# Fixed PSUM tiles for transposes, and an early load of the neighbourhood bias

## The chip, the cores and the metric

The kernel runs on one core of one Trainium2 chip. The metric is the device time of the whole program in microseconds (us), the median of the runs shown. Instructions run on five engines with a queue each: TensorE (PE in the profile; PEld is its weight load), VectorE (DVE), ScalarE (ACT), GpSimd (POOL) and SyncE (SP, which here issues all DMAs).

## What is computed

Two stacks of two transformer layers follow each other on 256 tokens of 1024 numbers, in float32. A layer of the first stack is a feed-forward, a mixer of four attentions, and a second feed-forward:

```python
for l in range(DEPTH):                       # DEPTH = 2
    h = rms_norm(x, ffn1_norm[l])
    x = x + 0.5 * swiglu(h, ffn1_w_gate[l], ffn1_w_up[l], ffn1_w_down[l])
    h = rms_norm(x, mix_norm[l])
    ...
    o_a = neighborhood_attention(na_q, na_k, na_v, ..., na_rel_bias[l], rows)
    o_b = diff_attention(...)
    o_c = gqa_axial_attention(...)
    o_d = dilated_attention(...)
    x = x + concatenate([o_a, o_b, o_c, o_d]) @ w_out[l]
    h = rms_norm(x, ffn2_norm[l])
    x = x + 0.5 * swiglu(h, ffn2_w_gate[l], ffn2_w_up[l], ffn2_w_down[l])
```

The neighbourhood attention adds a learned bias to its scores. The bias depends on the distance in rows and columns of a grid 64 wide, and only keys within a window of 16 columns count. A layer of the second stack is another mixer of three attentions and one feed-forward, with norms whose scale and shift come from a product of a vector with a large matrix ("modulation", loaded as `ada`).

## The kernel before

**Products.** Every weight matrix is streamed from HBM in units of 128 x 2048 numbers (`WStream`, lines 396 to 467). SP loads a unit into one of three buffers `raw`. ACT casts it to a rounded high part `whi`, and DVE subtracts to get the low part `wlo`; four pairs of them exist, and a unit is split when the fourth unit before it is done. PE then forms each product as three matmuls (`mm3`, line 625): high by high, low by high and high by low. So each load has a lead over its use of several units.

**Feed-forward** (`ffn`, line 641). The inner width of 2816 is done in 11 chunks of 256 (`NCH`). For each chunk and each half of the tokens, PE makes a gate and an up projection into one PSUM tile `mm` (two of them exist), ACT applies the gate function (`sil`), DVE multiplies (`hch`), PE transposes `hch` into a PSUM tile `tp` (`turn`, line 658), ACT and DVE split it into `hth` and `htl`, and the down projection of the chunk four before (`down`, line 671) accumulates into four PSUM tiles `y`. Between these steps `slot` advances background work: constants, a bias of the second stack, and the modulation, 192 loads of 256 KB `ada` with a DVE operation each.

**First kind of mixer** (`mixer1`, line 1088). `inproj` (line 1033) makes six chunks of projections. Each chunk of queries and keys goes through `prep` (line 847): ACT copies and squares, DVE sums, a power on POOL gives the norm's factor (`rs<-ms`), DVE scales and rotates, PE transposes into `tp`, ACT and DVE split that into `qkT`. When inputs are ready, jobs begin: `diff_job` (line 971, four heads) and `job` (line 903, two heads each of the dilated, grouped and neighbourhood attention, in this order). A job makes scores into PSUM tiles called `att` (they take slots of `y`, and of `mm` during the output projection), DVE takes maxima or adds a bias (`nm`, `e`), ACT exponentiates (`p`, `pd`), PE transposes through `tp` and multiplies by the values. `outproj` (line 1059) ends the mixer.

**The neighbourhood bias.** `na_bias` (line 826) takes four tiles `nab` of 128 x 512, one a head, and issues for each of them four loads on SP; a load fills 64 partitions with four runs of 64 numbers (256 bytes) each, 64 KB. `mixer1` calls it after the first two chunks of projections (`pre2`, line 1095). `na_bias_mask` (line 840) multiplies each tile by 8 and adds the mask of the window, one DVE operation a tile; it is a job of its own ahead of the two neighbourhood jobs (line 1135). `job` reads the tiles when it adds the bias (line 923).

**The order.** The kernel's Python code doesn't issue instructions at once. `Plan` (line 73) collects them with what each depends on (`add`, line 100), an estimated cost (`cost`, line 165: an issue on SP counts 475 ns) and the tiles with a limited number of slots that it touches. `order` (line 196) then simulates the five engines: of the operations that can start within 60 ns of the earliest, each engine takes the one of the highest priority, and `slot_time` (line 240) says whether the slots for the tiles of an operation are free and may be taken ahead of tiles that come earlier in the program. Priorities come from a pass from the end backwards, three times over (`priorities`, line 324). `issue` (line 318) emits the instructions in the order found. A DMA may not be issued ahead of the last matmul that stands before it in the program (line 136), the weight loads excepted. Each engine runs its own queue in that order and waits wherever an input is late, so a late input holds what is queued behind it.

**Tiles.** PSUM has eight banks: two `mm`, two `tp`, four `y`. `tp` (line 617) takes a tile of the pool's rotating slots. SBUF has 20 tiles `m` of 512 numbers (`NMID`) for all intermediate values, `nab` and `ada` among them.

```python
    def tp(self):
        return self.ps.tile([P, 512], F32, tag="tp", name="tp")
```

All instructions are emitted by `issue`, so they carry its line, L322, in the profile; they are told apart by the names of their tiles.

Of the kernel before, what the change touches and what calls it, by code (L numbers as in the profile page):

```python
# [72 lines left out]
class Plan:  # L73
# [3 lines left out]
    def __init__(self, nc):  # L77
        self.nc = nc
        self.ops, self.slot_of, self.slots = [], {}, {}
        self.write, self.read = {}, {}  # L80
        self.last_mm = self.cold = None
        self.lead = []
        for e in ("tensor", "vector", "scalar", "gpsimd", "sync"):
            setattr(self, e, Engine(self, e))
# [15 lines left out]
    def add(self, eng, method, args, kw):  # L100
# [4 lines left out]
        for writes in (False, True):  # L105
            for k, a in aps:
# [13 lines left out]
                if not writes:  # L120
                    if a.space == PSUM:
                        deps.update(j for j, _ in self.read[name] if self.ops[j][0] != eng)
# [42 lines left out]
    def cost(self, eng, method, args, kw, aps):  # L165
# [4 lines left out]
        psum = any(a.space == PSUM for _, a in aps)  # L170
# [25 lines left out]
    def order(self, prio):  # L196
# [43 lines left out]
        def slot_time(i):  # L240
# [3 lines left out]
            for t in ops[i][5]:  # L244
                if t not in live:
                    k = self.slot_of[t]
                    q = queue[k]
                    while head[k] < len(q) and q[head[k]] in done_alloc:
                        head[k] += 1
                    c = need.get(k, 0)  # L250
                    if free[k] <= c or place[t] > head[k] and max(held[k][head[k]:place[t]]) + c >= self.slots[k]:
                        return None
                    need[k] = c + 1
                    t0 = max(t0, sorted(freed_at[k])[c])
# [63 lines left out]
    def issue(self):  # L318
        for i in self.order(self.priorities())[0]:
            eng, method, args, kw = self.ops[i][:4]  # L320
            for m, a, k in args if method == "fused" else [(method, args, kw)]:
                getattr(getattr(self.nc, eng), m)(*a, **k)  # L322
# [147 lines left out]
class Net:  # L470
    def __init__(self, ctx, tc, A, out, stop):
# [20 lines left out]
        self.ps = pool("ps", 2, space=PSUM)  # L492
        self.mhalf = self.const.tile([P, 64], F32, name="mhalf")
# [123 lines left out]
    def tp(self):  # L617
        return self.ps.tile([P, 512], F32, tag="tp", name="tp")
# [22 lines left out]
    def ffn(self, ydone, mid, pre, r=None):  # L641
# [63 lines left out]
        for c in range(2, NCH):  # L705
            u = [W.next() for _ in range(2)]
# [381 lines left out]
    def mixer1(self, l, ydone, mid, pre):  # L1088
# [4 lines left out]
        bias = []  # L1093

        def pre2():
            pre()
            self.o = self.big.tile([P, 2, D], F32, tag="big", name="o")
            bias.extend(self.na_bias(l))
# [34 lines left out]
        for kind, vf, v0, g in (("dil", "v1", 4, 3), ("gqa", "vgqa", 8, 2), ("na", "vna", 10, 0)):  # L1133
            if kind == "na":
                self.jobs.append((lambda: True, lz(lambda: self.na_bias_mask(bias))))
# [409 lines left out]
    def run(self):  # L1545
# [28 lines left out]
        for i in range(n_phase):  # L1574
# [35 lines left out]
            else:  # L1610
                self.ffn(ydone, mid, pre, None if i else r0)
# [119 lines left out]
```

## Time and profile before

| | us |
|---|---|
| runs | 1606.23, 1602.98, 1605.62 |
| median | 1605.62 |
| the profiled execution | 1602.79 |
| its span, first to last instruction | 1601.0 |
| PE busy | 1583.4 |
| DVE busy | 1092.8 |
| ACT busy | 845.0 |

The profile shows one execution. Busy time of matmuls is modelled at their ends, as matmuls overlap. In the table of stages a line gives the stretch in us from the span's start, its length, and for PE, PEld, DVE, ACT and POOL the busy time with the count of instructions; then PE's granted clock (1.00 is the full 2.4 GHz), the busy share of the DMA engines and GB/s. A stage ends here with the last matmul of its kind: the first feed-forward at 197.3, the first mixer's projections and attention at 282.3 and its output projection at 320.3, then two feed-forwards to 694.3, the second mixer's projections and attention to 778.7. In a timeline, a line is start, duration, engine, operation, tile written and tiles read, the count of merged instructions, and in brackets the idle time of the engine before it with what ended it. PE's waits in the list of waits are totals, counts and the longest.

### The profile page before, as it was taken

The numbers are of one execution on the slowest core, as the hardware profiler recorded it, in microseconds if no ns is written. First come the engines' busy times: TensorE is split into PE (matmuls) and PEld (weight loads), VectorE is DVE, ScalarE is ACT, GpSimd is POOL, SyncE is SP. The second block draws the span as 40 slices with busy tenths as digits, with TensorE's granted clock in tenths as the row PEclk, the third lists the DMA queues.
The fourth block names the chain that finished last, engine by engine and source line by source line (L and its number), as shares of the span: only waits on it lengthen the run. The fifth ranks groups of instructions, "written<-read, shape, count | busy, mean of one in ns | idle before, by whom it ended". The sixth has DMA issues, their size and how long they took to land.

```text
span 1601.0 us, 21143 instructions
## 1 busy us (share of the span) xinstructions
PE 1583.4 (99%) x7792; PEld 1304.9 (82%) x7792; DVE 1092.8 (68%) x2034; ACT 845.0 (53%) x1438; POOL 128.6 (8%) x157
## 2 busy tenths in 40 slices
PE   9999999999999999999999999999999999999998
PEld 7888877788888888887788888888888888888886
DVE  6557789777778777689877755657645385585543
ACT  6554457654444544357654443766534368664442
POOL 0000043000000000033200000301000021000000
PEclk9999999999999999999999999999999999999999
DMA  8569762277777777763357744632654454165551
GB/s 311 215 231 322 277 222 88 106 296 280 291 269 264 294 272 294 291 224 111 132 210 308 272 161 160 215 132 93 239 208 169 168 199 173 65 224 184 176 194 51
DMA packets 81883, 335.77 MB, mean 210 GB/s; under 512 B 17136, under 2 KB 19700, under 8 KB 50676
## 3 DMA queue, kind: packets, MB, share of 16 engines
q1 hardware_dynamic: 81780, 334.42, 57.8%
q8 instruction: 61, 1.00, 0.2%
q14 instruction: 42, 0.34, 0.1%
HBM read 333.29 MB, written 2.84 MB: 210 GB/s over the span
## 4 chain that ended last, share of the span: by engine, by line
PE 89%; DVE 5%; ACT 2%; issue 1%; POOL 1%; DMA 0%; SPq 0%; DVEq 0%; POOLq 0%; ACTq 0%
PE mm L322 55%; PE y L322 27%; PE tp L322 5%; PE att L322 3%; DVE wlo L322 1%; POOL rs L322 1%; DVE nm L322 1%; ACT p L322 1%; DVE qk L322 0%; DVE p L322 0%; ACT whi L322 0%; DMA raw<-in_gu 0%; DVE pd L322 0%; DVE e L322 0%; DVE ss L322 0%
## 5 line engine op out<-in xcount | busy, mean ns | idle before, releaser
L322 DVE TENSOR_TENSOR wlo<-raw,whi 128x1024 fp32r<-128x1024 f32 (+2 forms) x516 | 604.4, 1204 | 245.6 <-ACT whi L322 242.6
L322 ACT CAST whi<-raw 128x1024 fp32r<-128x1024 f32 (+2 forms) x516 | 512.7, 1037 | 300.7 <-PE y L322 131.4
L322 PE MATMUL mm<-whi,xh 128*128 128x512 f32 (+2 forms) x1376 | 542.6, 394 | 1.9 <-ACT whi L322 1.2
L322 PE MATMUL mm<-wlo,xh 128*128 128x512 f32 (+2 forms) x1376 | 534.7, 389 | 0.7 <-DVE wlo L322 0.7
L322 PE MATMUL mm<-whi,xl 128*128 128x512 f32 (+2 forms) x1376 | 533.7, 389 | 0.7 <-DVE xl L322 0.7
L322 PEld LDWEIGHTS mm<-whi,xl 128*128 128x128 f32 x1376 | 258.6, 188 | 54.0 <-DVE xl L322 1.4
L322 PEld LDWEIGHTS mm<-whi,xh 128*128 128x128 f32 x1376 | 258.6, 188 | 53.0 <-ACT whi L322 2.0
L322 PEld LDWEIGHTS mm<-wlo,xh 128*128 128x128 f32 x1376 | 258.7, 188 | 50.4 <-DVE wlo L322 1.6
L322 PE MATMUL y<-whi,hth 128*128 128x512 f32 x528 | 205.9, 391 | 0.0
L322 PE MATMUL y<-whi,htl 128*128 128x512 f32 x528 | 205.6, 389 | 0.0
L322 PE MATMUL y<-wlo,hth 128*128 128x512 f32 x528 | 205.5, 389 | 0.0
L322 ACT ACTIVATE sil<-mm 128x256 f32<-128x256 f32 x110 | 42.3, 384 | 207.3 <-PE mm L322 206.5
L322 DVE CUSTOM_DVE_ANT_0 ada<-ada,act 128x512 f32<-128x512 f32 x192 | 128.1, 684 | 26.1 <-DMA ada<-in_ada 25.4
L322 POOL TENSOR_TENSOR rs<-rs,mhalf 128x1 f32<-128x1 f32 x28 | 25.6, 915 | 1223.5 <-DVE rs L322 1223.5
L322 PEld LDWEIGHTS y<-whi,htl 128*128 128x128 f32 x528 | 99.1, 188 | 20.7
L322 PEld LDWEIGHTS y<-whi,hth 128*128 128x128 f32 x528 | 99.1, 188 | 20.4 <-ACT whi L322 0.2
L322 PEld LDWEIGHTS y<-wlo,hth 128*128 128x128 f32 x528 | 99.1, 188 | 20.3
L322 DVE TENSOR_TENSOR hch<-mm,sil 128x256 f32<-128x256 f32 x110 | 46.3, 421 | 74.9 <-ACT sil L322 74.6
L322 POOL TENSOR_TENSOR rs<-ms,mhalf 128x2 f32<-128x2 f32 (+3 forms) x34 | 50.8, 1496 | 170.6 <-DVE ms L322 143.3
L322 DVE TENSOR_TENSOR htl<-tp,hth 128x512 fp32r<-128x512 f32 x66 | 45.0, 689 | 12.6 <-ACT hth L322 12.1
L322 PE MATMUL y<-wlo,oth 128*128 128x512 f32 x128 | 51.3, 401 | 0.0
L322 PE MATMUL y<-whi,oth 128*128 128x512 f32 x128 | 50.7, 400 | 0.0
(166 smaller groups left out, 1334.9 us busy)
## 6 DMA issues: line engine op xcount, KB each, us to landing
raw<-in_gu SPq DMA_DIRECT2D x127, 1024.0 KB, 4.9
raw<-in_dn SPq DMA_DIRECT2D x66, 1024.0 KB, 4.9
ada<-in_ada SPq DMA_DIRECT2D x192, 256.0 KB, 5.5
raw<-in_in SPq DMA_DIRECT2D x32, 1024.0 KB, 4.9
raw<-in_out SPq DMA_DIRECT2D x16, 1024.0 KB, 4.8
row<-moddram SPq DMA_DIRECT2D x12, 512.0 KB, 6.7
raw<-in_in2a SPq DMA_DIRECT2D x4, 840.0 KB, 4.4
raw<-in_gu SPq DMA_DIRECT2D x6, 512.0 KB, 5.2
```

The lines of the kernel that those rows point to most:

```text
L322: getattr(getattr(self.nc, eng), m)(*a, **k)
```

## The change

`tp` no longer takes a slot of the pool. Two PSUM tiles are made once (`fixed`), and `tp` returns a stand-in, a tile in another memory that is never accessed, with two slots for the planner. `issue` gives each stand-in a fixed tile at its first use, the one that came free first, and puts it back after the last use. `add` and `cost` treat a stand-in as PSUM. `slot_time` collects all new tiles of an operation per kind of slot and tests them together. `ffn` gets a hook `early`, called ahead of its ninth chunk; in the feed-forward in front of each mixer of the first kind it issues the bias loads and the masks, and `mixer1` uses the tiles from there.

```diff
--- before.py
+++ after.py
@@ -79,6 +79,8 @@
         self.ops, self.slot_of, self.slots = [], {}, {}
         self.write, self.read = {}, {}
         self.last_mm = self.cold = None
+
+        self.stand, self.fixed = {}, []
         self.lead = []
         for e in ("tensor", "vector", "scalar", "gpsimd", "sync"):
             setattr(self, e, Engine(self, e))
@@ -118,7 +120,7 @@
                 w = self.write[name]
                 deps.update(w[idx].tolist())
                 if not writes:
-                    if a.space == PSUM:
+                    if a.space == PSUM or name in self.stand:
                         deps.update(j for j, _ in self.read[name] if self.ops[j][0] != eng)
                     self.read[name].append((i, idx))
                     continue
@@ -167,7 +169,7 @@
         if method == "dma_start":
             return (1000 if eng == "gpsimd" else 475), 4 * int(np.prod(list(args[0].shape))) / 360, None
         n = max(int(np.prod(list(a.shape)[1:])) for k, a in aps)
-        psum = any(a.space == PSUM for _, a in aps)
+        psum = any(a.space == PSUM or a.tensor.name in self.stand for _, a in aps)
         if eng == "tensor":
             if method == "transpose":
                 return 109, 0, None
@@ -243,15 +245,18 @@
             need = {}
             for t in ops[i][5]:
                 if t not in live:
-                    k = self.slot_of[t]
-                    q = queue[k]
-                    while head[k] < len(q) and q[head[k]] in done_alloc:
-                        head[k] += 1
-                    c = need.get(k, 0)
-                    if free[k] <= c or place[t] > head[k] and max(held[k][head[k]:place[t]]) + c >= self.slots[k]:
+                    need.setdefault(self.slot_of[t], []).append(place[t])
+            for k, ps in need.items():
+                q = queue[k]
+                while head[k] < len(q) and q[head[k]] in done_alloc:
+                    head[k] += 1
+                if free[k] < len(ps):
+                    return None
+                ps.sort()
+                for j in range(head[k], ps[-1]):
+                    if j not in ps and held[k][j] + sum(1 for x in ps if x > j) > self.slots[k]:
                         return None
-                    need[k] = c + 1
-                    t0 = max(t0, sorted(freed_at[k])[c])
+                t0 = max(t0, sorted(freed_at[k])[len(ps) - 1])
             return t0
 
         done_alloc = set()
@@ -316,10 +321,30 @@
         return out, start, max(end)
 
     def issue(self):
-        for i in self.order(self.priorities())[0]:
+        order = self.order(self.priorities())[0]
+        uses = {}
+        for o in self.ops:
+            for t in o[5]:
+                uses[t] = uses.get(t, 0) + 1
+        free, got = list(self.fixed), {}
+
+        def real(a):
+            if not isinstance(a, bass.AP) or a.tensor.name not in self.stand:
+                return a
+            f = got[a.tensor.name]
+            return bass.AP(tensor=f.tensor, offset=f.offset + a.offset - self.stand[a.tensor.name].offset, ap=a.ap)
+
+        for i in order:
             eng, method, args, kw = self.ops[i][:4]
+            for t in self.ops[i][5]:
+                if t in self.stand and t not in got:
+                    got[t] = free.pop(0)
             for m, a, k in args if method == "fused" else [(method, args, kw)]:
-                getattr(getattr(self.nc, eng), m)(*a, **k)
+                getattr(getattr(self.nc, eng), m)(*[real(x) for x in a], **{n: real(x) for n, x in k.items()})
+            for t in self.ops[i][5]:
+                uses[t] -= 1
+                if t in self.stand and uses[t] == 0:
+                    free.append(got[t])
 
     def priorities(self):
 
@@ -490,6 +515,7 @@
         self.keep = pool("keep")
         self.sm = pool("sm", 4)
         self.ps = pool("ps", 2, space=PSUM)
+        nc.fixed = [self.ps.tile([P, 512], F32, name=f"tp{i}", bufs=1) for i in range(2)]
         self.mhalf = self.const.tile([P, 64], F32, name="mhalf")
         self.W = WStream(nc, raw_p, w_p, self.unit_specs())
         make_identity(tc.nc, self.ident)
@@ -615,7 +641,10 @@
         return self.mid_p.tile([P, 512], dt, tag="m", name=name)[:, :n]
 
     def tp(self):
-        return self.ps.tile([P, 512], F32, tag="tp", name="tp")
+
+        t = self.dram.tile([P, 512], F32, name="tpv", tag="tp", bufs=2)
+        self.nc.stand[t.tensor.name] = t
+        return t
 
     def split(self, hi, lo, src):
         self.nc.scalar.copy(hi, src)
@@ -638,7 +667,7 @@
             self.mm3(ps[:, :n], self.xh[:, k, tok], self.xl[:, k, tok], wh[:, c], wl[:, c], k == 0, k == 7)
 
 
-    def ffn(self, ydone, mid, pre, r=None):
+    def ffn(self, ydone, mid, pre, r=None, early=None):
         nc, W = self.nc, self.W
         hT, hs = {}, {}
         y = None
@@ -703,6 +732,8 @@
                 for t in range(2):
                     post(c, t, ps[t])
         for c in range(2, NCH):
+            if early and c == NCH - 3:
+                early()
             u = [W.next() for _ in range(2)]
             for t in range(2):
                 ps = mmps()
@@ -1090,12 +1121,11 @@
         self.flags, self.done, self.oT, self.half = set(), {}, {}, {}
         self.att_tag = ["y"]
         self.lam[l] = self.diff_lambda(l)
-        bias = []
+        bias = self.bias
 
         def pre2():
             pre()
             self.o = self.big.tile([P, 2, D], F32, tag="big", name="o")
-            bias.extend(self.na_bias(l))
 
         G = self.gain1[l]
         qkT = {}
@@ -1131,8 +1161,6 @@
             self.jobs.append((has("diff", "v1"), lz(lambda h=h: self.diff_job("diff", l, h, *([a[:, h // 2] for a in T] for T in qkT["diff"]), h, 256 + 64 * h))))
         diff_o = (lambda: self.done.get("diff", 0) == 4, lz(lambda: self.turn_o(1, "diff")))
         for kind, vf, v0, g in (("dil", "v1", 4, 3), ("gqa", "vgqa", 8, 2), ("na", "vna", 10, 0)):
-            if kind == "na":
-                self.jobs.append((lambda: True, lz(lambda: self.na_bias_mask(bias))))
             for f, hs in enumerate(((0, 2), (1, 3)) if kind == "gqa" else ((0, 1), (2, 3))):
                 def mk(kind=kind, v0=v0, g=g, f=f, hs=hs):
                     T = qkT[kind]
@@ -1608,7 +1636,12 @@
             if kind == 1:
                 (self.mixer1 if b == 1 else self.mixer2)(l, ydone, mid, pre)
             else:
-                self.ffn(ydone, mid, pre, None if i else r0)
+                def early():
+                    self.bias = self.na_bias(l)
+                    for _ in self.na_bias_mask(self.bias):
+                        pass
+
+                self.ffn(ydone, mid, pre, None if i else r0, early if b == 1 and kind == 0 else None)
 
 
 @with_exitstack
```

## Rows read from the trace of the kernel before

**Rows 1.** The page, busy time of each engine

```profile
PE 1583.4 (99%) x7792; PEld 1304.9 (82%) x7792; DVE 1092.8 (68%) x2034; ACT 845.0 (53%) x1438; POOL 128.6 (8%) x157
```

**Rows 2.** Busy time by stage

```profile
14.00:197.30 183.30, 183.30 (x833) 151.10 (x832) 120.92 (x181) 94.73 (x124) 2.15 (x2) 1.00 0.74 269
...
197.30:282.30 85.00, 82.27 (x479) 64.78 (x478) 78.32 (x199) 55.34 (x126) 32.86 (x26) 1.00 0.50 167
...
320.30:694.30 374.00, 373.76 (x1706) 309.38 (x1705) 278.92 (x487) 170.57 (x224) 3.50 (x4) 1.00 0.75 279
694.30:778.70 84.40, 81.12 (x479) 64.43 (x478) 78.87 (x201) 55.19 (x127) 33.12 (x26) 1.00 0.50 167
```

**Rows 3.** Busy time in the middle of the two mixers, same columns

```profile
231.40:273.00 41.60, 39.60 (x250) 29.77 (x246) 40.08 (x132) 30.08 (x83) 16.87 (x17) 1.00 0.24 89
...
728.00:770.00 42.00, 38.72 (x247) 29.30 (x247) 40.84 (x132) 31.02 (x84) 18.57 (x17) 1.00 0.29 101
```

**Rows 4.** Who PE waits for, whole span, first line

```profile
PE tp L322 <- DVE qkT L322: 2.7, 2, 1.8
```

**Rows 5.** Groups of instructions, the masks: busy us, mean ns, idle before

```profile
L322 DVE SCALAR_TENSOR_TENSOR nab<-nab,namask 128x512 f32<-128x512 f32 x8 | 5.5, 712 | 0.0
```

**Rows 6.** Timeline of DVE, mixer of layer 0

```profile
229.59 0.68 DVE L322 SCALAR_TENSOR_TENSOR nab<-nab,namask 128x512 f32<-128x512 f32 x1
...
230.53 0.68 DVE L322 SCALAR_TENSOR_TENSOR nab<-nab,namask 128x512 f32<-128x512 f32 x1
231.40 1.23 DVE L322 TENSOR_TENSOR wlo<-raw,whi 128x1024 fp32r<-128x1024 f32 x1 [0.20 <-ACT whi L322]
232.55 1.28 DVE L322 TENSOR_REDUCE nm<-att 128x2 f32<-128x512 f32 x2
```

**Rows 7.** Timeline of ACT, mixer of layer 0

```profile
230.32 2.00 ACT L322 CAST whi<-raw 128x1024 fp32r<-128x1024 f32 x2 [0.69 <-PE mm L322]
```

**Rows 8.** Timeline of DVE, mixer of layer 1

```profile
713.27 0.93 DVE L322 SCALAR_TENSOR_TENSOR nab<-nab,namask 128x512 f32<-128x512 f32 x1
...
720.97 1.89 DVE L322 SCALAR_TENSOR_TENSOR nab<-nab,namask 128x512 f32<-128x512 f32 x3
...
723.90 1.22 DVE L322 TENSOR_TENSOR wlo<-raw,whi 128x1024 fp32r<-128x1024 f32 x1 [0.71 <-ACT whi L322]
```

**Rows 9.** Timeline of POOL, mixer of layer 1

```profile
714.37 3.82 POOL L322 TENSOR_TENSOR rs<-ms,mhalf 128x16 f32<-128x16 f32 x1 [0.71 <-DVE ms L322]
```

**Rows 10.** Timeline of SP, late first feed-forward and first mixer

```profile
169.53 0.33 SPq L322 DMA_DIRECT2D raw<-in_in  x1
...
203.19 11.71 SPq L322 DMA_DIRECT2D nab<-nad  x15
216.86 0.35 SPq L322 DMA_DIRECT2D raw<-in_in  x1
```

**Rows 11.** DMAs in 200 to 217 us, and (last line) in 120 to 140

```profile
q1 hardware_dynamic: 4526, 3.62, 74.0%
...
nab<-nad SPq DMA_DIRECT2D x15, 64.0 KB, 2.7
...
ada<-in_ada SPq DMA_DIRECT2D x9, 256.0 KB, 7.9
```

**Rows 12.** Timeline of DVE and PE around 270 us, mixer of layer 0

```profile
269.58 0.28 DVE L322 TENSOR_TENSOR qkT<-tp,qkT 128x128 fp32r<-128x128 f32 x1
...
270.00 0.63 PE L322 MATMUL tp<-ident,p 128*128 128x128 f32 x4 [0.98 <-DVE qkT L322]
...
271.71 0.68 DVE L322 TENSOR_TENSOR otl<-tp,oth 128x512 fp32r<-128x512 f32 x1
```

**Rows 13.** The chain of waits, first feed-forward: start, us, what

```profile
129.61 5.49 PE mm L322 x24
135.10 5.44 PE y L322 x24
```

## The prediction

> **What bounds the kernel now.** I read the busy table first, then the engines' busy time by stage, then who PE waits for, and last the timelines of DVE, POOL, PE and SP around the places that the change touches. PE is busy 1583.4 us of a span of 1601.0 [rows 1], so at most 17.6 us are to be had without less matrix work, and the change removes no matmul. The rest is unevenly spread over the stages [rows 2]: the first feed-forward leaves PE no gap at all (183.30 of 183.30), the two between the first mixers leave 0.24 in 374.00. The attention part of the first kind of mixer, from its first projection to its output projection, leaves 85.00 - 82.27 = 2.73 us in layer 0 and 84.40 - 81.12 = 3.28 in layer 1. The granted clock is 1.00 of 2.4 GHz in each of these rows, so no stage has clock to win back.
>
> Inside those two stretches the gaps sit where DVE is full: DVE works 40.08 of 41.60 us and 40.84 of 42.00 while PE loses 41.60 - 39.60 = 2.00 and 42.00 - 38.72 = 3.28 [rows 3]. PE's longest waits for another engine's work are transposes that wait for DVE to read the transposed queries and keys out of PSUM, 2.7 us in two waits [rows 4]. So the one thing that time can be taken from here is DVE work in, or just ahead of, these stretches.
>
> **The change part by part.**
>
> *Masks off DVE in the mixer.* Eight mask operations, four a layer, have a mean of 0.712 us [rows 5]; in a run of them DVE starts one about each 0.6 us (three take 1.89) [rows 8]. They move from the first quarter of the mixer into the feed-forward ahead, where DVE has room. What they are worth depends on what ends the stretch that they stand in. In layer 0 the last two stand at 229.59 and 230.53; behind them DVE idles 0.20 us for ACT's cast of a weight tile, goes on with that tile's low part at 231.40 and comes to the maxima of the differential attention at 232.55 [rows 6]. The cast had waited for PE [rows 7], so the low part does not move up. The two maxima can, by at most the two masks, 2 x 0.6 = 1.2 us, if the order puts them ahead of that low part; as DVE is full from there on and PE loses 2.00 us to it, I take the whole 1.2. In layer 1 the first mask stands at 713.27, just ahead of the means of squares that POOL's power waits for, and POOL idles 0.71 us for them [rows 8, 9]; that power leads through the normalized queries and keys, their transposes and ACT's copies to the cast behind which DVE's full stretch begins at 723.90. I take that 0.71. The other three end at 722.86, where DVE then idles 0.71 us for the cast [rows 8]: 0. Bounds for all eight: 0, and 8 x 0.6 = 4.8, which is under the 2.00 + 3.28 that PE loses. Taken: 1.9.
>
> *Sixteen bias loads a layer off SP's queue in the mixer, into the ninth chunk of the feed-forward.* Fifteen of them hold SP for 11.71 us [rows 10], 0.78 each, 12.5 for sixteen. The weight load behind them goes out at 216.86, 1.96 us after the fifteenth was issued, so it waited for something else (a free buffer), and taking the loads out of the mixer gains 0. In the feed-forward they go past the weight loads and the 256 KB loads of the modulation, on the same queue. What covers them is the lead of the weights: the mixer's first weight load is issued at 169.53 [rows 10] and the feed-forward's last matmul ends at 197.3, some 27 us later. A delay of 12.5 us in issuing fits in that; the DMA engines' own work for them is less than their busy time in a stretch that holds fifteen of them, 74.0% of 17 us = 12.6 us, all other loads included [rows 11]. I take 0; the ends are 0 and the 6.8 us of the second rival. With the cover gone the uncovered part would fall on PE whole, as PE has no gap there.
>
> The Trainium skill speaks against this move: "DMA: Bandwidth & Descriptors", sections Specifications and Bandwidth, wants runs of at least 512 bytes and transfers near 1 MiB, and calls transfers under 64 KB dominated by descriptors; these are 64 KB in runs of 256 bytes. By its table a 64 KB load occupies the engines 0.95 us, 16 x 0.95 = 15.2 us a layer (an estimate from that page, which measured another queue); with the rule at its full weight the second rival would be likelier than I make it.
>
> *Two fixed PSUM tiles for the transposes.* There are two slots before and two after; the operations and the planner's rules for those slots are the same, but which slot a tile gets is now settled in the order of issue, the one that came free first. This could only pay if PE now waited for one slot while the other stood empty. At the wait that ends at 270.00 it did not: DVE reads the queries' and keys' tile out at 269.58 and the other tile, the differential output's, at 271.71 [rows 12], so both were held by late DVE work, and PE got the one that came free first. I take 0; ends: the two waits of 2.7 us in all gone, or doubled.
>
> *The planner's test for free slots.* It now lets one operation take two slots that stand behind each other in the queue of tiles. Fused score matmuls take two, but in the attention stretches there are four to choose from, and the test differs only with two later tiles already live. With the masks gone the planner writes a new order for the mixers in any case. What another order is worth I take from the two layers, which run the same code in two orders: 85.00 against 84.40 us [rows 2], so 0.6 a mixer either way, 1.2 for both. I take 0.
>
> *Sum.* -1.9 us against the profiled execution: 1602.79 - 1.9 = 1600.9. That execution lies 2.83 us under the median of the runs, 1605.62, on which the forecast is made: 1605.62 - 1.9 = 1603.7. A measurement of this kernel can tell about 0.2%, 3.2 us, from no change, so this is **no change** that can be seen.
>
> **The rivals.**
>
> *A, faster: the new order ends DVE's backlog.* The masks' 2.4 us a layer, and the freedom to place other DVE work where they stood, reach the full stretches in both layers. For it: DVE's 96 to 97% there, and that PE's long waits in them are for DVE. Against it: the idle times of 0.20 and 0.71 us between the masks and these stretches, which show that DVE had caught up. It gives at most the 2.00 + 3.28 = 5.28 us: 1605.62 - 5.28 = 1600.3.
>
> *B, slower: the masks wait for their loads in DVE's queue in the feed-forward.* The ninth chunk of layer 0 lies around 130 us. A 256 KB modulation load lands there 7.9 us after its issue; the bias loads in the mixer landed after 2.7 [rows 11]. The planner charges SP 0.475 us for an issue, and 0.78 is measured, so DVE may come to a mask early and stand still, with the products of gate and up projection behind it; those free the two PSUM tiles that PE writes next. PE's cover is one projection and one down projection, 5.49 + 5.44 = 10.9 us [rows 13]. If DVE stood still from the first issue to the last landing, 12.5 + (7.9 - 2.7) = 17.7 us, PE would lose 17.7 - 10.9 = 6.8: 1605.62 + 6.8 = 1612.4. It decides from a DVE standstill of 10.9 us on. Against it: the masks stand among other DVE work, so the wait comes in four pieces, and SP's issues are not in one run where weight loads come between.
>
> *C: it does not happen.* The order of the program only says from where on the loads may be issued; if the planner still puts loads and masks into the mixer, nothing changes: 1605.6.
>
> **How the numbers follow.** The forecast's own case has 0.49, A 0.32, B 0.13, C 0.06. Under the forecast's case an order better or worse by more than the layers differ leaves 0.03 faster and 0.04 slower. So faster 0.30 of A and 0.03 = 0.33; slower 0.12 of B and 0.04 = 0.16; the same 0.51. The range reaches to A's full gain, 1600.3, and up to half of B's price, 1605.62 + 3.3 = 1608.9; the forecast's own range is 1601.5 to 1606.5.
>
> **What would show it.** Right: masks and bias loads of layer 0 between 124 and 197 us, no new PE gap there; DVE still full in the middle of both mixers; PE's idle time in the two attention stretches about 4 us in sum instead of 6.0. A: that sum under 2 us, with no PE transpose waiting for DVE for over 0.5 us. B: a DVE wait of several us for a bias load in a feed-forward, with PE matmuls waiting behind a gate product, and PE no longer busy all of 14 to 197. Wrong altogether: a change in the second block's mixers or feed-forwards, which hold none of the moved work, or weight tiles that come late to PE.

## The result, and the profile after

The changed kernel takes **1613.45 us** (median of four runs, 1612.09 to 1613.80) against 1604.39 for the kernel before (four runs): ratio 1.0053, 95% interval 1.0040 to 1.0065. It is 9 us slower; the forecast was 1603.7, and the range ended at 1608.9. The profiled execution took 1613.80 us, its span 1612.0. All instructions are emitted in one line of the code again, now L343.

Busy time by stage of the changed kernel, in the columns of [rows 2]; the first line is a short stretch at the start of the program, the last three are short stretches inside the mixers:

```profile
10.20:13.61 3.41, 3.41 (x12) 2.94 (x11) 3.33 (x9) 3.41 (x9) 0.00 (x0) 0.50 1.04 404
14.00:198.50 184.50, 184.50 (x839) 151.87 (x838) 120.25 (x182) 94.20 (x124) 1.10 (x2) 1.00 0.75 265
198.50:289.47 90.97, 84.65 (x479) 67.06 (x477) 81.49 (x198) 55.76 (x126) 32.80 (x26) 0.96 0.45 165
327.45:701.48 374.03, 373.79 (x1707) 309.39 (x1706) 281.62 (x491) 170.56 (x224) 3.50 (x4) 1.00 0.77 282
701.48:787.45 85.97, 81.47 (x479) 65.05 (x478) 76.74 (x194) 55.53 (x125) 30.99 (x26) 1.00 0.43 156
787.45:827.05 39.60, 38.61 (x221) 30.04 (x222) 22.86 (x70) 24.49 (x60) 3.62 (x4) 0.96 0.14 50
201.35:204.76 3.41, 3.30 (x8) 2.62 (x9) 3.41 (x6) 2.98 (x6) 0.00 (x0) 0.50 1.01 414
245.72:249.13 3.41, 3.41 (x15) 2.60 (x13) 3.26 (x12) 2.82 (x11) 2.50 (x3) 0.50 0.32 132
788.44:791.85 3.41, 3.41 (x16) 3.21 (x16) 0.91 (x4) 0.72 (x2) 0.00 (x0) 0.50 0.26 106
```

The same view of the kernel before, output projection of the second mixer:

```profile
778.76:816.01 37.25, 37.07 (x223) 28.58 (x223) 27.20 (x70) 25.52 (x58) 3.64 (x4) 1.00 0.27 93
```

Against [rows 2], projections and attention take 90.97 - 85.00 = 5.97 us more in layer 0 and 85.97 - 84.40 = 1.57 more in layer 1, whose output projection takes 39.60 - 37.25 = 2.35 more. The first feed-forward ends 1.2 us later, and that hangs mostly on the start of the program, where the granted clock was 0.50 from 10.20 to 13.61: x1 and x10, whose profiled executions have such a stretch there too, end this stage at 198.7 and 198.3, x6 and x13, which have none, at 197.1 and 197.3. In sum that is 11.1 us; the two profiled executions are 11.0 apart, and the stages between and behind are as they were. In layer 1's attention DVE does less, 76.74 us against 78.87, as planned, and PE still loses more. In three stretches inside the mixers, 3.41 us each, the granted clock is 0.50, the 1.2 GHz level. PE had waited ahead of each (2.49, 0.53 and 1.96 us). Matmuls of 128x512 that follow each other start 0.43 us apart in the first of them, and 0.23 us apart at a granted clock of 1.00. So a stretch that PE works through costs up to half its length, 1.7 us (an estimate from these numbers), and the three up to some 5 of the 11 us.

Who PE waits for in the changed kernel, its two longest rows:

```profile
PE mm L343 <- DVE xl L343: 3.6, 3, 2.5
PE y L343 <- ACT p L343: 3.4, 2, 2.0
```

The transposes' wait of [rows 4] is gone, and these two took its place: the split of the normalized input at the start of a mixer, and the exponentials ahead of the output projection.

### The profile page after: what moved, and what is told of

Read it like the earlier page. It is cut to its first block, busy times and chain, and to the rows that moved or that the text cites. A ratio compares the mean times of both kernels' runs of the same rounds, so it can differ in the third digit from the quotient of the medians.

```text
span 1612.0 us, 21097 instructions
## 1 busy us (share of the span) xinstructions
PE 1589.7 (99%) x7792; PEld 1311.2 (81%) x7792; DVE 1093.3 (68%) x2034; ACT 844.4 (52%) x1438; POOL 125.2 (8%) x157
## 3 DMA queue, kind: packets, MB, share of 16 engines
q1 hardware_dynamic: 81780, 334.42, 57.2%
## 4 chain that ended last, share of the span: by engine, by line
PE 89%; DVE 6%; ACT 2%; issue 1%; POOL 1%; DMA 0%; SPq 0%; POOLq 0%; DVEq 0%; ACTq 0%
PE mm L343 54%; PE y L343 27%; PE tp L343 5%; PE att L343 3%; DVE wlo L343 2%; POOL rs L343 1%; ACT p L343 1%; DVE qk L343 0%; DVE nm L343 0%; DVE e L343 0%; ACT whi L343 0%; DVE p L343 0%; ACT pd L343 0%; DVE qkT L343 0%; DMA raw<-in_gu 0%
## 5 line engine op out<-in xcount | busy, mean ns | idle before, releaser
L343 DVE TENSOR_TENSOR wlo<-raw,whi 128x1024 fp32r<-128x1024 f32 (+2 forms) x516 | 605.6, 1208 | 241.9 <-ACT whi L343 241.2
L343 ACT CAST whi<-raw 128x1024 fp32r<-128x1024 f32 (+2 forms) x516 | 512.3, 1037 | 308.1 <-PE mm L343 125.6
L343 PE MATMUL mm<-whi,xh 128*128 128x512 f32 (+2 forms) x1376 | 544.9, 396 | 1.6 <-ACT whi L343 0.9
L343 PE MATMUL mm<-whi,xl 128*128 128x512 f32 (+2 forms) x1376 | 535.4, 390 | 3.6 <-DVE xl L343 3.6
L343 PE MATMUL mm<-wlo,xh 128*128 128x512 f32 (+2 forms) x1376 | 535.9, 390 | 0.3 <-DVE wlo L343 0.2
L343 PEld LDWEIGHTS mm<-whi,xl 128*128 128x128 f32 x1376 | 259.7, 189 | 57.6 <-DVE xl L343 5.1
L343 PEld LDWEIGHTS mm<-whi,xh 128*128 128x128 f32 x1376 | 260.2, 189 | 51.9 <-ACT xh L343 1.4
L343 PEld LDWEIGHTS mm<-wlo,xh 128*128 128x128 f32 x1376 | 260.0, 189 | 50.7 <-DVE wlo L343 1.1
L343 PE MATMUL y<-whi,hth 128*128 128x512 f32 x528 | 205.9, 391 | 0.0
L343 PE MATMUL y<-whi,htl 128*128 128x512 f32 x528 | 205.7, 390 | 0.0
L343 PE MATMUL y<-wlo,hth 128*128 128x512 f32 x528 | 205.5, 389 | 0.0
L343 DVE CUSTOM_DVE_ANT_0 ada<-ada,act 128x512 f32<-128x512 f32 x192 | 129.3, 691 | 34.2 <-DMA ada<-in_ada 34.2
L343 ACT ACTIVATE sil<-mm 128x256 f32<-128x256 f32 x110 | 42.3, 384 | 203.9 <-PE mm L343 203.1
L343 POOL TENSOR_TENSOR rs<-rs,mhalf 128x1 f32<-128x1 f32 x28 | 24.5, 876 | 1226.8 <-DVE rs L343 1226.8
L343 PEld LDWEIGHTS y<-whi,htl 128*128 128x128 f32 x528 | 99.1, 188 | 21.1 <-DVE htl L343 0.3
L343 PEld LDWEIGHTS y<-wlo,hth 128*128 128x128 f32 x528 | 99.2, 188 | 20.3
L343 PEld LDWEIGHTS y<-whi,hth 128*128 128x128 f32 x528 | 99.0, 188 | 20.3 <-ACT whi L343 0.2
L343 DVE TENSOR_TENSOR hch<-mm,sil 128x256 f32<-128x256 f32 x110 | 46.4, 422 | 71.1 <-ACT sil L343 70.7
L343 POOL TENSOR_TENSOR rs<-ms,mhalf 128x2 f32<-128x2 f32 (+3 forms) x34 | 48.5, 1430 | 155.4 <-DVE ms L343 150.3
L343 PE MATMUL y<-whi,oth 128*128 128x512 f32 x128 | 51.7, 408 | 4.2 <-ACT p L343 3.4
L343 DVE TENSOR_TENSOR htl<-tp,hth 128x512 fp32r<-128x512 f32 x66 | 45.0, 690 | 12.7 <-ACT hth L343 12.2
L343 PE MATMUL y<-wlo,oth 128*128 128x512 f32 x128 | 51.1, 399 | 0.0
```

Of the source, the lines that this page charges most:

```text
L343: getattr(getattr(self.nc, eng), m)(*[real(x) for x in a], **{n: real(x) for n, x in k.items()})
```

## The start of layer 0's mixer: followed back

Timeline of the changed kernel: SP in the feed-forward, then DVE, then PE at the start of the mixer:

```profile
129.68 9.67 SPq L343 DMA_DIRECT2D nab<-nad  x8
139.45 0.55 SPq L343 DMA_DIRECT2D ada<-in_ada  x1
140.09 0.38 SPq L343 DMA_DIRECT2D raw<-in_gu  x1
...
141.72 6.56 SPq L343 DMA_DIRECT2D nab<-nad  x8
...
189.51 0.69 DVE L343 CUSTOM_DVE_ANT_0 ada<-ada,act 128x512 f32<-128x512 f32 x1 [3.18 <-DMA ada<-in_ada]
...
190.13 1.28 DVE L343 SCALAR_TENSOR_TENSOR x<-y,x 128x512 f32<-128x512 f32 x2
...
200.72 1.28 DVE L343 TENSOR_TENSOR xl<-tp,xh 128x512 fp32r<-128x512 f32 x2
...
201.46 0.79 PE L343 MATMUL mm<-whi,xl 128*128 128x512 f32 x1 [2.49 <-DVE xl L343]
```

The same places in the kernel before:

```profile
131.26 0.33 SPq L322 DMA_DIRECT2D raw<-in_gu  x1
...
184.19 0.69 DVE L322 CUSTOM_DVE_ANT_0 ada<-ada,act 128x512 f32<-128x512 f32 x1 [4.10 <-DMA ada<-in_ada]
...
184.91 1.37 DVE L322 SCALAR_TENSOR_TENSOR x<-y,x 128x512 f32<-128x512 f32 x2
```

The sixteen loads hold SP for 9.67 + 6.56 us, and a weight load goes out at 140.09 in place of 131.26. While SP is at the first eight, the DMA engines are at first busy throughout, and at the end little over half, at 81 GB/s (two stretches in the columns of [rows 2]; the last two numbers are the DMA engines' share, 1 when all are busy, and GB/s):

```profile
132.00:135.00 3.00, 3.00 (x14) 2.47 (x14) 3.00 (x7) 1.58 (x2) 0.00 (x0) 1.00 1.03 418
137.00:139.45 2.45, 2.45 (x13) 2.02 (x12) 0.67 (x3) 0.00 (x0) 0.00 (x0) 1.00 0.56 81
```

At the feed-forward's end DVE stands at a modulation operation until its load has landed, with the first residual next in its queue. Before, it stood there 4.10 us already. Now the residual comes at 190.13 in place of 184.91; everything that prepares the mixer's input follows it, and PE waits 2.49 us for the low part `xl`. That DVE stood at the bias tiles themselves, as the second rival had it, is not so:

```profile
DVE nab L343 <- DMA nab<-nad: 1.5, 2, 1.1
```

## Experiments

Several kernels have their order written out: `issue` takes a list of the operations in place of the planner's result,

```diff
-        order = self.order(self.priorities())[0]
+        order = listed(ORDER)
```

and the text says which list. Theories: **1**, SP's hold by the loads delays what PE needs at the start of the mixer; **2**, the planner's new order of the mixers is worse by itself. Ratios are to the kernel before, run on the same chip.

**x1 and x2: the two parts alone.** x1 keeps the fixed tiles and the new slot test; x2 keeps the early loads with the new slot test, and takes the transposes' tiles from the pool.

```diff
x1:
-                self.ffn(ydone, mid, pre, None if i else r0, early if b == 1 and kind == 0 else None)
+                self.ffn(ydone, mid, pre, None if i else r0, None)
x2:
     def tp(self):
-        t = self.dram.tile([P, 512], F32, name="tpv", tag="tp", bufs=2)
-        self.nc.stand[t.tensor.name] = t
-        return t
+        return self.ps.tile([P, 512], F32, tag="tp", name="tp")
```

> The two fixed PSUM tiles and the new test for free slots, with the bias loads and masks left in the mixer; the order of every engine is that of the kernel before. Theory 1 (the sixteen loads on SP's queue delay the weights) and theory 2 (the planner's new order of the mixer is worse) both expect no change: ratio 1.000, within 0.998 to 1.002. The rival that the fixed tiles themselves cost (a transpose waits for its own tile while the other is free) expects the whole loss, about +9 us, ratio 1.005.

> The early bias loads and masks with the new test for free slots, but the transposes' tiles from the pool's rotating slots; the order of every engine is that of the changed kernel. Theories 1 and 2 both expect the changed kernel's time, 1612 to 1615 us, ratio about 1.005. The rival that the fixed tiles cost expects the time of before, ratio 1.000. If fixed tiles help under the new order, this kernel is slower than the changed one, over 1615 us.

x1: 1602.71 us, ratio 1.0000 (0.9990 to 1.0009). x2: 1612.48, ratio 1.0059 (1.0044 to 1.0074). The fixed tiles cost and bring nothing; the early bias, with the new order that it brings, carries the whole loss.

**x3 and x4: place and order apart.** x3 has loads and masks early and the rest in the order of before; x4 has them in the mixer and the rest in the order of the changed kernel (both with fixed tiles and a written order).

> Loads and masks early, at the places among SP's and DVE's instructions that they have in the changed kernel; all other instructions in the order of the kernel before. Theory 1 (SP's hold of 9.7 and 6.6 us delays the weight stream, mixer 1 of layer 0 starts with late splits) expects most of the loss here: PE waits over 2 us at the start of the first mixer, +4 to +9 us, ratio 1.0025 to 1.0055. Theory 2 (the new order) expects nothing or the forecast's gain: 1601 to 1606 us, ratio 0.998 to 1.000.

> Loads and masks in the mixer, at the places among SP's and DVE's instructions that they have in the kernel before; all other instructions in the order of the changed kernel. Theory 2 expects most of the loss here: PE waits of 1.5 to 2 us ahead of both output projections, +5 to +9 us, ratio 1.003 to 1.0055. Theory 1 expects no loss: ratio 1.000.

x3: 1608.15 us, ratio 1.0032 (1.0020 to 1.0045). x4: 1610.46, ratio 1.0049 (1.0034 to 1.0064). Each costs something by itself, 4.9 and 7.3 us. Busy time of projections and attention in x3, layers 0 and 1:

```profile
200.10:287.67 87.57, 82.53 (x480) 64.76 (x479) 78.27 (x198) 55.32 (x126) 31.93 (x26) 1.00 0.45 165
699.55:783.80 84.25, 81.07 (x479) 64.56 (x478) 76.54 (x197) 54.87 (x127) 33.11 (x26) 1.00 0.44 156
```

In x3 the loss is in layer 0 alone: 87.57 - 85.00 = 2.57 us here, and 200.10 - 197.30 = 2.80 in the feed-forward ahead. About 1 of the latter lies at the start of the program again, where the granted clock was 0.50 from 9.75 to 13.16; two waits of PE for DVE, 0.34 us at 161.84 and 0.66 at 185.77, are another 1.0, so the loads reach PE in the feed-forward too. In layer 1 the loads hold SP too, 5.62 + 5.59 us by its timeline, but DVE then waits 0.79 us for PE ahead of the residual, so that the late modulation load is no longer what it waits for last. The masks' removal from the mixer shows in layer 1 as 84.40 - 84.25 = 0.15 us. x4 loses 87.12 - 85.00 = 2.1 us in layer 0 and 88.46 - 84.40 = 4.1 in layer 1 by the same view; a stretch of 3.41 us at a granted clock of 0.50 lies in each of the two (at 241.61 and 733.13), by the estimate above up to 1.7 us of each loss. PE ahead of the two output projections in x4:

```profile
285.40 0.50 PE L343 MATMUL y<-whi,oth 128*128 128x512 f32 x1 [1.45 <-ACT p L343]
...
785.88 0.50 PE L343 MATMUL y<-whi,oth 128*128 128x512 f32 x1 [1.95 <-ACT p L343]
```

**x5 and x6: the loads on another queue.** POOL issues the bias loads, in the changed kernel (x5) and in x3 (x6).

```diff
             eng, method, args, kw = self.ops[i][:4]
+            if method == "dma_start" and "nab" in args[0].tensor.name:
+                eng = "gpsimd"
```

> The changed kernel, every engine's order as it is, but the sixteen bias loads of each layer are issued by POOL instead of SP. Theory 1 (their hold of SP, 9.7 and 6.6 us, delays the weight and modulation loads) expects the PE wait of 2.5 us at the start of layer 0's first mixer gone and its projections and attention 2.5 to 4 us shorter than the changed kernel's 90.9: 1608 to 1610 us, ratio 1.003 to 1.004. The rival that the loads' own traffic of short runs delays the weights, whoever issues them, expects no change from the changed kernel: 1611 to 1614 us, ratio 1.005 to 1.006.

> As x3 (loads and masks early, all else in the order of the kernel before), but the sixteen loads of each layer are issued by POOL. Theory 1 expects x3's loss of 4.9 us gone: 1602 to 1604.5 us, ratio 0.999 to 1.001; the masks' removal would show as a ratio under 1.000 by at most 0.001. The rival of the loads' own traffic expects x3's 1608 us, ratio 1.003.

x5: 1610.23 us, ratio 1.0039 (1.0026 to 1.0052). x6: 1603.84, ratio 1.0001 (0.9991 to 1.0011). On POOL's queue x3's loss is gone. x6 keeps the masks in the feed-forward and holds the four `nab` tiles at least as early as x3, so neither of these is the cost. But the loads themselves are not the same: POOL issues them earlier, and they move in larger packets. POOL in x6, and the packets, MB and share of the two queues over the whole program (q1 is SP's, q0 POOL's):

```profile
105.91 2.65 POOL L345 DMA_DIRECT2D nab<-nad  x4 [85.50 <-PE y L345]
...
112.29 7.35 POOL L345 DMA_DIRECT2D nab<-nad  x12 [3.74 <-PE tp L345]
...
q1 hardware_dynamic: 73076, 332.32, 57.1%
q0 software_dynamic: 1024, 2.10, 0.7%
```

In x3 SP issues them from 129.67 to 149.38, some 24 us later, and its queue has 81780 packets; 17137 packets of x3 are under 512 bytes, 8944 of x6, where POOL's have 2 KB each. So x5 and x6 show that the cost hangs on the loads' being issued on SP at that place. Whether SP's time, the traffic of short packets or the later place makes it, they don't tell apart, and no other run does: while SP was at the loads, the DMA engines were full for most of the time (1.03 above), and at the end not (0.56). The prediction had weighed the rule on short runs. Another sentence of the Trainium skill, "DMA: Bandwidth & Descriptors", section Rules for kernel authors, is that issuing from several engines only saves the issuing sequencer's time. By it SP's time would be what was short; no run here shows that apart from the packets. Projections and attention in x6, layer 0:

```profile
197.08:282.66 85.58, 82.40 (x478) 64.79 (x478) 76.27 (x196) 55.29 (x126) 31.99 (x26) 1.00 0.44 160
```

**x7: the maxima ahead of the low parts.** In the changed kernel DVE makes two low parts of an output weight, then the last grouped scores' maxima; ACT's exponentials wait for those, and PE for the tiles that they free. Timeline of the changed kernel, layer 1 (DVE, ACT, PE):

```profile
782.63 2.36 DVE L343 TENSOR_TENSOR wlo<-raw,whi 128x1024 fp32r<-128x1024 f32 x2
784.89 1.29 DVE L343 TENSOR_REDUCE nm<-att 128x2 f32<-128x512 f32 x2
...
786.37 0.47 ACT L343 ACTIVATE p<-att,nm 128x256 f32<-128x256 f32 x1 [2.85 <-DVE nm L343]
...
787.45 0.50 PE L343 MATMUL y<-whi,oth 128*128 128x512 f32 x1 [1.96 <-ACT p L343]
```

The list of DVE's order is edited in both layers:

```diff
-wlo wlo (one output weight tile)
 nm nm nm nm (maxima of the last grouped scores, and their scaling)
+wlo wlo (one output weight tile)
```

> The changed kernel with one edit in DVE's order in each mixer: the two low parts of a weight tile that stand ahead of the last grouped scores' maxima come behind them. Theory 2 (PE waits 1.45 and 1.96 us ahead of the output projections, because those maxima hold the PSUM tiles that it writes) expects these waits gone: 1.5 us less in each layer and perhaps a half-clock stretch less, 1607 to 1610 us, ratio 1.0025 to 1.004. The rival that DVE is full there, and the low parts then hold PE as long, expects no change: 1611 to 1614 us, ratio 1.005 to 1.006.

1613.04 us, ratio 1.0053 (1.0038 to 1.0069): nothing is won. PE in x7, layer 1:

```profile
782.41 0.50 PE L343 MATMUL y<-whi,oth 128*128 128x512 f32 x1 [0.73 <-ACT p L343]
...
785.39 0.81 PE L343 MATMUL tp<-ident,p 128*128 128x128 f32 x4 [1.57 <-DVE p L343]
```

The wait at the projection falls from 1.96 to 0.73, and the next transposes wait 1.57 for DVE. A single wait is not the cost: whichever of the two comes first on DVE, PE waits for the other. The four runs differ: 1609.13 us at a mean granted clock of 1.000, the other three 1612.37 to 1614.26 at 0.996 to 0.997. One kernel thus differs by 3 to 5 us between executions, and its mean clock with it.

**x8: another order with nothing moved.** The kernel before, with the planner's window of choice narrowed:

```diff
-ITERS, DELTA, LATE = 3, 60, 20000
+ITERS, DELTA, LATE = 3, 40, 20000
```

> The kernel before, nothing moved, but the planner may pick among operations that can start within 40 instead of 60 ns of the earliest, so that it writes another order. If the loss by the order is what any new order of these mixers may cost, this is slower than before by 2 to 8 us, ratio 1.001 to 1.005. The rival that the early bias tiles make the order worse expects the time of before: ratio 0.999 to 1.001.

1609.55 us, ratio 1.0037 (1.0024 to 1.0050). PE in x8's two mixers, and the stretches at a lower clock that begin there, in the columns of [rows 2]:

```profile
245.06 1.09 PE L322 MATMUL tp<-ident,pd 128*128 128x128 f32 x4 [1.41 <-DVE pd L322]
...
743.57 1.11 PE L322 MATMUL tp<-ident,pd 128*128 128x128 f32 x4 [1.58 <-DVE pd L322]
...
245.00:248.41 3.41, 3.35 (x10) 2.76 (x11) 3.41 (x13) 2.17 (x8) 0.00 (x0) 0.50 0.25 99
743.34:746.75 3.41, 3.19 (x12) 2.79 (x13) 3.41 (x10) 1.46 (x5) 0.00 (x0) 0.50 0.24 96
```

Nothing was moved or removed, and another order costs 5.5 us, with its waits in other places. At both waits the granted clock falls to 0.50 for 3.41 us, by the estimate above up to 3.4 of the 5.5 us; all six runs have a mean clock of 0.995 or 0.996, the sixteen of the kernel before beside them 0.996 to 1.000. So the order costs by its waits and by the clock that falls at them.

**x9: the loads one by one.** As x3, but each load follows one of sixteen successive weight loads (another list).

> Loads and masks in the feed-forward, all else in the order of the kernel before, and the loads stay on SP; but they no longer stand in two blocks of eight: each follows one of sixteen successive weight loads, and the masks follow singly. Theory 1 in the form that a block of loads starves the weight stream expects no loss: 1602 to 1605 us, ratio 0.999 to 1.001. In the form that SP's time itself is short, wherever it is taken, it expects x3's loss: 1606.5 to 1609 us, ratio 1.002 to 1.0035.

1606.13 us, ratio 1.0019 (1.0009 to 1.0028), between the two expectations. Without blocks the residual is late all the same; DVE in x9:

```profile
187.59 0.69 DVE L343 CUSTOM_DVE_ANT_0 ada<-ada,act 128x512 f32<-128x512 f32 x1 [4.75 <-DMA ada<-in_ada]
```

So the blocks alone are not the point: spread, the loads still cost 2.6 us.

**x10: no masks at all.**

```diff
             eng, method, args, kw = self.ops[i][:4]
+            if method == "scalar_tensor_tensor" and "nab" in args[0].tensor.name:
+                continue
```

> The kernel before in its own order, with the eight masks left out (the neighbourhood scores then carry the unscaled bias without the window): the most that taking them off DVE in the mixer can bring. The forecast's term expects 1.9 us less: 1601 to 1602.5 us, ratio 0.9985 to 0.999. The rival that they lie beside other work wholly expects no change: ratio 0.9995 to 1.0005.

1603.16 us, ratio 0.9998 (0.9989 to 1.0007). PE's two waits for transposed queries and keys are where [rows 4] had them:

```profile
270.88 0.63 PE L324 MATMUL tp<-ident,p 128*128 128x128 f32 x4 [0.98 <-DVE qkT L324]
...
767.47 0.63 PE L324 MATMUL tp<-ident,p 128*128 128x128 f32 x4 [1.76 <-DVE qkT L324]
```

The time that the masks leave is idle time of DVE: it waits 1.57 us for ACT's cast at 232.29 in layer 0 and 1.21 at 724.72 in layer 1, where it waited 0.20 and 0.71 before [rows 6, 8]. POOL doesn't idle the 0.71 us of [rows 9] any more, but the cast doesn't come earlier for it. x10 keeps the order, so it can't show what the masks' removal is worth where the maxima stand ahead of that tile's low part.

**x11 to x13: another order of the changed kernel.** `DELTA` is 80 in all three. x11 issues the bias loads on POOL, x12 on SP; x13 has x11's order with loads and masks back in the mixer (a list, loads on SP).

> The changed kernel with POOL issuing the bias loads, as x5, and another order from the planner (it may pick among operations that can start within 80 instead of 60 ns of the earliest). If the loss by the order is the luck of one order, another order gives another time: anywhere from 1601 to 1612 us, and a time under 1607 shows that the early tiles leave good orders open. The rival that the early tiles make every order worse expects x5's time or more: 1609 to 1612 us, ratio 1.003 to 1.005.

> The changed kernel with x11's order, the bias loads issued by SP as the change has them. If SP's hold costs what it costs under the other orders (x3 against x6: 4.3 us; the changed kernel against x5: 2.6 us), this is 2 to 5 us over x11: 1603 to 1606 us, ratio 0.9995 to 1.0015. The rival that under this order PE doesn't wait for the late weights expects x11's time: 1600 to 1602.5 us, ratio 0.998 to 0.999.

> x11's order of all other instructions, but loads and masks in the mixer, where the kernel before has them among SP's and DVE's instructions. If x11's gain is the order's alone, and the early bias is worth nothing, this takes x11's time: 1600 to 1602.5 us, ratio 0.998 to 0.999. If DVE's time in the mixer, freed of masks, is what this order lives on, it is slower than x11 by one or two us or more: over 1602.5 us, ratio over 0.999.

x11: **1600.87 us, ratio 0.9982 (0.9973 to 0.9991)**, faster than both kernels, and 9.4 us under x5 (ratio 1.0039), from which only its order differs. x12: 1605.15, 1.0010 (0.9999 to 1.0021). x13: 1602.78, 0.9993 (0.9983 to 1.0002). Projections and attention in x11, then x13, layers 0 and 1, and PE at the start of x12's first mixer:

```profile
198.73:282.69 83.96, 81.74 (x478) 64.91 (x478) 77.23 (x194) 55.40 (x126) 32.10 (x26) 1.00 0.44 161
694.82:776.60 81.78, 80.92 (x479) 64.87 (x478) 75.51 (x193) 54.99 (x125) 33.37 (x26) 1.00 0.44 160
```

```profile
197.33:281.94 84.61, 81.77 (x479) 64.82 (x478) 79.36 (x196) 55.47 (x126) 32.78 (x26) 1.00 0.49 166
694.07:777.63 83.56, 81.44 (x480) 64.76 (x478) 77.82 (x197) 55.51 (x125) 32.86 (x26) 1.00 0.50 169
```

```profile
200.67 0.50 PE L343 MATMUL mm<-whi,xl 128*128 128x512 f32 x1 [2.17 <-DVE xl L343]
```

The loads on SP cost 4.3 us here as well (x12 against x11). Whether the early bias has a part in x11's gain stays open: x13 without it is 1.9 us slower, and its stretch in layer 1 takes 83.56 - 81.78 = 1.78 us more, but the two intervals overlap.

**x14: the late modulation load out of the residual's way.** As x3, with four operations moved in DVE's list:

```diff
-ada ada ada
 x x (first residual)
-ada
 rs hn hn wlo wlo
+ada ada ada ada
```

> As x3 (loads and masks early on SP, all else in the order of the kernel before), with one more edit, on DVE alone, in the first feed-forward of layer 0: the four modulation operations next to the first residual come behind the normalization and the next weight tile's low part. If SP's hold reaches PE through the modulation load that DVE waits for ahead of the residual (2.50 us of idle time in x3, 4.10 before), x3's loss goes: PE's wait at the start of the mixer under 1 us, its projections and attention under 86.2 us in place of 87.6, 1603 to 1606 us, ratio 0.9995 to 1.0015. The rival that the weight tiles themselves come too late expects x3's time: 1607 to 1609 us, ratio 1.002 to 1.0035.

1605.96 us, ratio 1.0013 (1.0003 to 1.0023): half of x3's loss is gone, and the stretch of layer 0 takes 86.79 us (expected under 86.2, or 87.6). DVE, then PE, in x14:

```profile
185.32 1.39 DVE L343 SCALAR_TENSOR_TENSOR x<-y,x 128x512 f32<-128x512 f32 x2 [2.00 <-PE y L343]
...
198.58 1.28 DVE L343 TENSOR_TENSOR xl<-tp,xh 128x512 fp32r<-128x512 f32 x2
...
199.32 0.50 PE L343 MATMUL mm<-whi,xl 128*128 128x512 f32 x1 [1.11 <-DVE xl L343]
```

The residual waits for PE alone now, but the moved operations stand ahead of `xl`. The load's way through DVE's queue is thus shown for about half; that the rest is these operations' own time was not tried.

One measure puts the runs in line: the time from the first residual to the feed-forward's end, against PE's wait for `xl` right after it.

| kernel | residual starts | feed-forward ends | between | PE waits |
|---|---|---|---|---|
| before | 184.91 | 197.3 | 12.4 | 0 |
| x5 (POOL) | 187.87 | 199.2 | 11.3 | 0 |
| x11 (POOL) | 187.69 | 198.7 | 11.0 | 0 |
| x6 (POOL) | 186.11 | 197.1 | 11.0 | 0 |
| x7 (SP) | 188.11 | 197.8 | 9.7 | 1.20 |
| x9 (SP, spread) | 188.21 | 197.4 | 9.2 | 1.68 |
| x3 (SP) | 191.14 | 200.1 | 9.0 | 1.91 |
| x12 (SP) | 189.34 | 198.0 | 8.7 | 2.17 |
| changed (SP) | 190.13 | 198.5 | 8.4 | 2.49 |
| x2 (SP) | 191.07 | 199.2 | 8.1 | 2.72 |

Under some 11 us, every microsecond less is a microsecond of PE's. x14 stands outside this line, with 12.4 us between and a wait of 1.11, as its moved operations stand between. The kernel before had 12.4 - 11.0 = 1.4 us to spare.

## Why the prediction was wrong

- **The order, taken at 0 with 0.6 a mixer either way: the term that failed most.** It came from two layers that run the same code. In orders without SP's loss that stretch ran from 83.96 to 87.20 us in layer 0 (x11, x8) and from 81.78 to 88.46 in layer 1 (x11, x4): several times 0.6. Two draws from one plan say little on the next plan. Theory 2 is confirmed by x4 and x8, in the form that an order is luck, not that the early tiles spoil it (x11). Part of that luck is the clock: each of these stretches of x4 and x8 holds one of 3.41 us at a granted clock of 0.50, up to 1.7 us of it.
- **The loads on SP, taken at 0 under a cover of "some 27 us": failed.** That lead was the weights'. The same queue carries the modulation loads, and one of them had no lead: DVE stood 4.10 us for it in the kernel before, with the residual next. Measured: 4.9 us (x3), 0 on POOL (x6), 4.3 (x12). What on SP's queue makes the load late, the time of issuing or the short packets, stays open. The second rival's price, 6.8, was near by luck; its mechanism, masks that wait for their loads, was not what happened (1.5 us in all).
- **The masks, taken at -1.9: failed.** Leaving them out of the kernel before brings a ratio of 0.9998 (x10). The waits at which PE loses time do not move with them. In both layers DVE waits longer for the cast instead (1.57 us in place of 0.20, 1.21 in place of 0.71), and the 0.71 us of [rows 9] bring that cast no earlier. The 1.2 us of layer 0 had a condition, maxima ahead of the low part, that x10's order doesn't meet. Under x11's order the early bias may be worth as much as the forecast's 1.9 us (x13), but that is inside the two intervals.
- **The fixed tiles, taken at 0: right** (x1).
- **"No stage has clock to win back": right, but one could lose it.** Three stretches at half clock made up to some 5 of the 11 us in the profiled execution, by the estimate above; the prediction had no term for that.
- **The signs.** The feed-forward has no new gap of PE (184.50 of 184.50 us), as forecast, but PE's idle time in the two stretches is 6.32 + 4.50 = 10.8 us where about 4 was forecast. The first rival's sign, under 2 us with no transpose waiting over 0.5, came true in no run: x11 is nearest, with 2.22 + 0.86 = 3.1 us and a transpose that waits 1.18.

The parts don't add: 4.9 (x3) and 7.3 (x4) make 12.2, the whole is 9.1. A stretch of half clock more or less in a run, and waits that overlap, may account for that; it was not taken apart further.

## What to carry to other kernels

Before work is put on a queue, read every stream of that queue for the one with no lead: a consumer that already idles for its load, with the critical operation next in line, has a cover of 1 or 2 us, whatever the others have. When loads are moved to another queue as a test, look there at when they are issued and in what packets: both changed here. Where a planner writes the order, an edit draws a new one: run a few orders of both versions (one constant does it) before the edit is judged, as the spread of orders, 9 us here, hides an effect of 2. Masks or other small work that is moved off a full engine pay only where the wait that ends the stretch moves with them.

## What was not expected of the hardware

The granted clock falls to 0.50 after some short waits of PE in the middle of the program, and not after others: in the changed kernel at 201.35 (a wait of 2.49 us) and at 788.44 (1.96), while x5 kept 1.00 after a wait of 1.97 at the place of the second, x12 after 2.17 at the place of the first, and the kernel before after 1.76, where x1, in the same order, fell to 0.50 at 767.88 after 1.66. So a wait of 2 us can cost up to 1.7 us more by the estimate above, in some executions of a kernel and not in others (x7). A bias load of 64 KB held SP for 0.58 us when it stood alone (x9), and between 0.70 us (5.62 for eight, x3, layer 1) and 1.2 us (9.67 for eight) in a block; what sets this was not tried.
